# Ten Strassen pairs in place of seven, with the gates of four attention units among their blocks, and running states by scans

## The chip, the cores and the metric

The kernel runs on one core of a Trainium2 chip. The metric is the device time of one execution in microseconds. It was run three times: 1944.55, 1938.79 and 1942.80 us, median 1942.8. One further execution was profiled.

## The reference

One layer of a streaming encoder step is computed for a prompt of 1024 tokens and for 8 samples of 16 tokens, 1152 tokens in all (`NT`), with shared weights. The model width is 1024. Cut to what matters here:

```python
h = rms_norm(x, norm_g) * (1 + scale) + shift
proj = h @ w_in                       # one projection, 11296 columns
q, k, v, z_att, z_ssd, xbc, dt_raw, gates = split(proj)
q, k = rms_norm per head of 64
o_att = chunk-band attention (16 heads; own chunk of 64 + 8 chunks back; clipped relative bias)
att_branch = (o_att * silu(z_att)) @ w_att_proj
x, B, C = split(silu(causal_dwconv(xbc)))
for each chunk:                       # 32 heads of 64, 4 groups, state of 128
    y = (C B^T * decay) (x dt) + C h exp(a_cs)
    h = h * exp(a_cs_end) + B^T (x dt to_end)
ssd_branch = group_rms_norm((y + D x) * silu(z_ssd)) @ w_ssd_proj
merged = sigmoid(g_att) * att_branch + sigmoid(g_ssd) * ssd_branch
out = x + gate * (merged @ w_out)
```

The column ranges used below are `z_att` (1024 columns, 8 blocks of 128, one for each attention unit of two heads), `z_ssd` (2048 columns, 16 blocks, one for each pair of SSD heads) and `gates` (2048 columns, 16 blocks).

## The kernel before

All products are made in split single precision: an operand is a high part and a low part, and a product is three matmuls (high by high, high by low, low by high). A block of 128 columns of `w_in` for all tokens ("dense", the function `dense`) is 8 steps along the width x 3 groups of 384 tokens x 3 matmuls (L489, L490, L492) = 72 matmuls of 384 columns. The weights of a block arrive in one 512 KB load into one of two raw buffers (L350, issued by SyncE) and are split by ACT (high part, L374) and VectorE (low part, L375).

Two blocks can be made together by Strassen's scheme (`pairs`, with its weight forms in `w_form`): 7 products in place of 8 half-size ones, each with 24 matmuls of 288 columns (L880, L882, L883). `AHEAD_BLOCKS` lists the blocks that are made ahead of attention. The stages, in the order of time:

1. Start: normalisation, the conversion of the input into operands, the first block (`z_att` of unit 0) and four gate blocks dense (`NZ` = 5 blocks).
2. Seven pairs (`NPR`), the z blocks 0 to 13 of the SSD branch, then block 14 dense. Finished blocks go to HBM (`keep_block` into `z_d` or `gate_d`).
3. Eight attention units (`attention(u)`). A unit projects q, k and v token by token (`dense_tok`): 9 tiles of 128 tokens x 8 steps x 3 matmuls (L555 to L557), with 384 columns, in the last unit 416. The three weight pieces of a unit have one place: a piece's place comes free when the unit before has used it for the last time. Then comes one dense block, `z_att` of the next unit. The norms of q and k are made by POOL in three steps of 4, 4 and 1 token tiles (`prelude`: L1228, the Newton steps L328 to L334, and the product L1232), then the tiles are transposed on TensorE (L1252, L1268). Beside the projection of the next unit run the prompt rounds of this unit (scores L1390, transposes L1311, weighted sums L1334) and the sample's (L1443, L1446, L1470, L1480).
4. The SSD stage: four groups; in each a B and a C block with convolution, then four pairs of heads (`ssd(p)`). A pair has its x block (dense, convolution on VectorE, L1531), transposes L1754, eight chunk state products of 128x128 (L1799), the chain of running states, the in-chunk products (L1830) and those of the samples (L1837), the state output (L1855) and the sample's states (L1881). The chain of running states is fourteen operations of 64 columns on VectorE (L1808: state times decay plus the chunk's product; the first chunk is a copy on ACT, L1804), two for each chunk because a pair holds two heads. Seven further dense blocks are placed between pairs by the table `SLOTS` (z block 15 and gates 4 to 9).
5. The last six gate blocks, and the products with `w_att_proj`, `w_ssd_proj` and `w_out`.

What stands where is set in two steps. The program is written by generators: `run` lets the dense generators give a few matmuls at a time, counts the time that they are worth on a clock (`clock`, `credit`), and lets the other work in between, when its `pause` and `until` have passed. Then the Tile scheduler puts the instructions of each engine in an order by its own timeline. Instructions wrapped in `late` keep their program order. Each engine's queue is executed in order.

Of the kernel before, what the change touches and what calls it, by code (L numbers as in the profile page):

```python
# [12 lines left out]
P = 128  # L13
# [8 lines left out]
HD = 64  # L22
# [9 lines left out]
NEARLY = 15  # L32
SLOTS = (('p', 1), ('p', 3), ('p', 6), ('p', 9), ('p', 11), ('p', 13), ('p', 15))
BLOCKS = [("gate", i) for i in range(4)] + [("z", p) for p in range(NPAIR)] + [("gate", i) for i in range(4, 16)]
AHEAD_BLOCKS = BLOCKS[:4 + NEARLY]
FILL = dict(zip(SLOTS, BLOCKS[4 + NEARLY:]))
NGATE = 4 + NEARLY + len(SLOTS) - NPAIR
NZ = 5
NPR = 7
# [92 lines left out]
def trunk_kernel(ctx: ExitStack, tc: tile.TileContext, h):  # L132
# [118 lines left out]
    L_SSD = marena.set_layout(Z0, [("X", 1, XW), ("R", 2, 1184), ("t", 8, 36), ("pad", 1, 576), ("T", 9, NT), ("Y", 1, 1184), ("H", 1, 1024),  # L251
# [72 lines left out]
    z_d = drp.tile([1 + NPAIR, P, NT], F32, name="z_d")  # L324
# [17 lines left out]
    def job(*raw):  # L342
        jobs.append([len(parts) + i for i in range(len(raw))])
        parts.extend(raw)
# [119 lines left out]
    jobs_att = [len(jobs)]  # L464
    for u in range(NU - 1):
        job(*(h["wall"][nz + 4 * u + i] for i in range(3)))
        job(h["wall"][nz + 4 * u + 3])
    job(*(h["wlast"][i] for i in range(4)))
    jobs_att.append(len(jobs))
    for x in [h["wall"][i] for i in range(nz + 4 * NU - 4, 85)] + [h["watt"][i] for i in range(8)] + [h["wssd"][i] for i in range(16)] \  # L470
            + [h["wout"][i] for i in range(8)]:
        job(x)
# [538 lines left out]
    def keep_block(n, z):  # L1011
        what, i = AHEAD_BLOCKS[n - 1]
        dma(gate_d[i] if what == "gate" else z_d[1 + i], z.ap)
# [11 lines left out]
    def do(what, *x):  # L1025
        if what == "first":
            ev_z(z[0], late)(0, x[0], groups[x[0]], first[x[0]])
            if x[0] == 2:
                dma(z_d[0], z[0].ap)
                z[0].free()  # L1030
# [53 lines left out]
    def pause(t):  # L1084
        yield from until(clock[0] + t)
# [89 lines left out]
    def attention(u):  # L1175
# [4 lines left out]
        def dense_gen():  # L1180
            qk = yield from walloc(lay, "Q", 16 * P)
            if u == 0:
                turn = alloc(lay, "T", NT)
                z = zs[0] = alloc(lay, "T", NT)
                dma(z.ap, z_d[0])
                turn.free()
# [29 lines left out]
            yield from dense(hops, ev_z(z))  # L1216
# [329 lines left out]
    def dt_gen():  # L1546
# [36 lines left out]
        nc.scalar.activation(dec, pe[:, :256], AF.Exp)  # L1583
# [31 lines left out]
    ngate = [max(4, 4 + NEARLY - NPAIR)]  # L1615

    def fill_dense(*slot):
# [5 lines left out]
        def ev(o, g, tok, ps):  # L1623
# [3 lines left out]
            store(z_d[1 + i][:, tok], t.ap)  # L1627
# [57 lines left out]
    def ssd(p):  # L1685
# [7 lines left out]
        e4 = dec.rearrange("p (c e) -> p c e", e=32)  # L1693
# [43 lines left out]
        def main():  # L1737
# [54 lines left out]
            xm = [masked(0), masked(1)]  # L1792

            yield from pause(1500)
            for j in range(2):
                ps = pg()
                for s in range(4):
                    c = 4 * j + s
                    nc.tensor.matmul(ps[:, s * P:(s + 1) * P], tokb.ap[:, c * P:(c + 1) * P], xw.ap[:, c * P:(c + 1) * P],  # L1799
                                     start=True, stop=True)  # L1800
                for s in range(4):
                    c = 4 * j + s
                    if c == 0:
                        nc.scalar.activation(hst.ap[:, 0:P], ps[:, 0:P], AF.Copy)  # L1804
                        continue
                    for e in range(2):
                        o = c * P + e * HD
                        nc.vector.scalar_tensor_tensor(  # L1808
                            hst.ap[:, o:o + HD], hst.ap[:, o - P:o - P + HD], e4[:, c, 2 * p + e:2 * p + e + 1],
                            ps[:, s * P + e * HD:s * P + e * HD + HD], ALU.mult, ALU.add)  # L1810
                yield 4 * 213
                yield from pause(900)
            xw.free()
# [4 lines left out]
            yield from pause(1200)  # L1818
# [23 lines left out]
            dma(z.ap, z_d[1 + p])  # L1842
# [371 lines left out]
```

## Time and profile before

| | |
|---|---|
| runs | 1944.55, 1938.79, 1942.80 us; median 1942.8 |
| profiled execution | 1943.42 us, its span in the trace 1941.6 us |
| mean granted TensorE clock | 0.999 |
| HBM | 202.72 MB read, 53.68 MB written |

In the trace a start is counted from the start of the span. Busy time is the time in which an engine has at least one instruction in work. Matmuls are pipelined: the duration of one (some 340 ns with 384 columns) is longer than the step from one to the next, and it is the step that counts. A wait line reads: engine, tile and line that waited, the engine, tile and line waited for, the total in us, how many times, the longest. A group line reads: line, engine, operation, written tile, read tiles, shape, count, then busy time and mean ns of one, then idle time of the engine ahead of it and what ended it. A timeline line is start, duration, engine, line, operation. The window lines give length, then busy time and count for each engine asked for, granted clock, the DMA engines' busy share and GB/s. The trace counts a matmul of the language as one or two records (L1830 and L1334 two, the 384-column ones one).

### The profile page before, as it was taken

To read this page: it belongs to the slowest core of one execution; us is meant where nothing else is said; L and a number is where in the kernel's file an instruction comes from. 1 tells how busy PE (TensorE), PEld (TensorE's weight loads), DVE (VectorE), ACT (ScalarE), POOL (GpSimd) and SP (SyncE) were. 2 spreads that over 40 slices of the span, in tenths; PEclk is the share of its full clock that TensorE was granted. 3 is DMA by queue.
4 is the path that set the end of the run, shared out by engine and by line. 5 is a ranking of instruction groups with operands and counts; after the bars stand their busy time and mean duration, and the time that the engine had idled before them with its cause. 6 is when DMAs were issued, how large, how long until landed. Compare 5 with 4: busy or idle time off the path is not lost.

```text
span 1941.6 us, 35765 instructions
## 1 busy us (share of the span) xinstructions
PE 1922.7 (99%) x14259; PEld 1842.4 (95%) x14259; DVE 1251.5 (64%) x2577; ACT 798.3 (41%) x1639; POOL 339.7 (17%) x615
## 2 busy tenths in 40 slices
PE   7999999999999999999999999999999999999999
PEld 5999999999899998998999999999999999999999
DVE  6756634555556456558597988888885434777732
ACT  7533324444454444545655546465453311111200
POOL 0000003213123131221022343242241300000000
PEclk9999999999999999999999999999999999999999
DMA  8222342343333333423345354554558742331341
GB/s 316 92 81 95 109 173 69 96 129 116 97 117 101 122 116 94 130 82 115 119 132 181 132 162 152 168 173 140 160 192 289 292 144 93 105 105 56 89 143 52
DMA packets 85966, 258.73 MB, mean 133 GB/s; under 512 B 14732, under 2 KB 15768, under 8 KB 85800
## 3 DMA queue, kind: packets, MB, share of 16 engines
q1 hardware_dynamic: 77416, 229.57, 36.5%
q0 software_dynamic: 8384, 26.88, 3.6%
q8 instruction: 112, 1.84, 0.4%
q14 instruction: 54, 0.44, 0.1%
HBM read 202.72 MB, written 53.68 MB: 132 GB/s over the span
## 4 chain that ended last, share of the span: by engine, by line
PE 92%; DVE 3%; DMA 2%; ACT 1%; issue 1%; POOL 0%; SPq 0%; ACTq 0%; DVEq 0%; POOLq 0%
PE d L489 11%; PE d L492 11%; PE d L490 11%; PE d L557 5%; PE d L555 5%; PE d L556 5%; PE s L489 4%; PE s L490 4%; PE s L492 4%; PE g L1311 3%; PE g L1334 3%; PE s L1390 2%; PE g L880 2%; PE g L883 2%; PE g L882 2%; PE g L490 1%
## 5 line engine op out<-in xcount | busy, mean ns | idle before, releaser
L489 PE MATMUL d<-rarena 128*128 128x384 f32 x1288 | 437.7, 340 | 0.0
L492 PE MATMUL d<-rarena 128*128 128x384 f32 x1288 | 434.2, 337 | 0.0
L490 PE MATMUL d<-rarena 128*128 128x384 f32 x1288 | 433.3, 336 | 0.0
L489 PEld LDWEIGHTS d<-rarena 128*128 128x128 f32 x1288 | 242.0, 188 | 4.1 <-issue 2.7
L492 PEld LDWEIGHTS d<-rarena 128*128 128x128 f32 x1288 | 241.9, 188 | 2.2 <-issue 2.0
L490 PEld LDWEIGHTS d<-rarena 128*128 128x128 f32 x1288 | 242.1, 188 | 0.8 <-issue 0.4
L557 PE MATMUL d<-va_att,rarena 128*128 128x384 f32 (+1 forms) x567 | 197.6, 349 | 0.0
L555 PE MATMUL d<-va_att,rarena 128*128 128x384 f32 (+1 forms) x567 | 196.7, 347 | 0.0
L556 PE MATMUL d<-va_att,rarena 128*128 128x384 f32 (+1 forms) x567 | 193.7, 342 | 0.0
L374 ACT ACTIVATE rarena<-arena 128x1024 fp32r<-128x1024 f32 x76 | 80.5, 1059 | 262.9 <-PE s L490 173.9
L489 PE MATMUL s<-rarena 128*128 128x384 f32 x488 | 165.6, 339 | 0.0
L490 PE MATMUL s<-rarena 128*128 128x384 f32 x488 | 164.2, 336 | 0.0
L492 PE MATMUL s<-rarena 128*128 128x384 f32 x488 | 163.3, 335 | 0.0
L1299 ACT ACTIVATE ma_att<-ma_att 128x640 f32<-128x640 f32 (+2 forms) x144 | 101.5, 706 | 135.8 <-DVE ma_att L1408 99.7
L1228 POOL TENSOR_SCALAR ma_att<-ma_att 128x16 f32<-128x16 f32 (+1 forms) x24 | 5.2, 218 | 707.3 <-DVE ma_att L1205 417.2
L557 PEld LDWEIGHTS d<-va_att,rarena 128*128 128x128 f32 x567 | 107.0, 189 | 3.9 <-issue 2.7
L555 PEld LDWEIGHTS d<-va_att,rarena 128*128 128x128 f32 x567 | 106.8, 188 | 2.7 <-issue 1.2
L375 DVE TENSOR_TENSOR rarena<-arena,rarena 128x1024 fp32r<-128x1024 f32 x76 | 93.3, 1227 | 22.6 <-ACT rarena L374 22.6
L556 PEld LDWEIGHTS d<-va_att,rarena 128*128 128x128 f32 x567 | 106.8, 188 | 0.5
L1531 DVE SCALAR_TENSOR_TENSOR ma_att<-ma_att,arena 128x1176 f32<-128x1176 f32 x63 | 93.9, 1491 | 9.4 <-ACT ma_att L1528 8.1
L489 PEld LDWEIGHTS s<-rarena 128*128 128x128 f32 x488 | 91.7, 188 | 1.3 <-issue 1.2
L490 PEld LDWEIGHTS s<-rarena 128*128 128x128 f32 x488 | 91.7, 188 | 0.8 <-issue 0.8
(437 smaller groups left out, 4128.0 us busy)
## 6 DMA issues: line engine op xcount, KB each, us to landing
arena<-in_wall_dram SPq DMA_DIRECT2D x85, 512.0 KB, 3.6
ma_att<-in_kc_dram SPq DMA_DIRECT2D x64, 256.0 KB, 4.3
ma_att<-in_vc_dram SPq DMA_DIRECT2D x64, 256.0 KB, 3.5
ma_att<-acs_d SPq DMA_DIRECT2D x23, 576.0 KB, 6.8
ma_att<-y_d SPq DMA_DIRECT2D x15, 576.0 KB, 6.3
arena<-in_wssd_dram SPq DMA_DIRECT2D x16, 512.0 KB, 4.5
z_d<-va_start SPq DMA_DIRECT2D x13, 576.0 KB, 2.8
ma_att<-eacs_d SPq DMA_DIRECT2D x26, 288.0 KB, 3.9
```

What stands on the lines that cost most here:

```text
L374: keep(nc.scalar.activation(hi.r[:, c], b.ap, AF.Copy))
L375: keep(nc.vector.tensor_tensor(lo.r[:, c], b.ap, hi.ap[:, c], ALU.subtract))
L489: nc.tensor.matmul(ps, hi.r[:, wc], kh.r[:, tok], start=k == 0, stop=False)
L490: nc.tensor.matmul(ps, hi.r[:, wc], kl.r[:, tok], start=False, stop=False)
L492: nc.tensor.matmul(ps, lo.r[:, wc], kh.r[:, tok], start=False, stop=k == nk - 1)
L555: nc.tensor.matmul(ps, kh.r[:, tok], wh, start=j == 0, stop=False)
L556: nc.tensor.matmul(ps, kh.r[:, tok], wl, start=False, stop=False)
L557: nc.tensor.matmul(ps, kl.r[:, tok], wh, start=False, stop=j == KT - 1)
L1299: nc.scalar.activation(p, p, AF.Exp, bias=sm_[:, 4 + e:5 + e], scale=-1.0, accum_out=sm_[:, 6 + e:7 + e])
L1311: nc.tensor.transpose(ps[:, s * P:(s + 1) * P], p[:, (j + s) * P:(j + s + 1) * P], ident)
L1334: late(nc.tensor.matmul(po[e * HD:e * HD + HD, a * P:(a + 1) * P], v.ap[:, vc:vc + HD], x.ap[:, o + i * P:o + (i + 1) * P], start=i == 0, ...
L1531: nc.vector.scalar_tensor_tensor(yc, r.ap[:, j:j + n], w4[:, i, j:j + 1], yc, ALU.mult, ALU.add)
```

## The change

Blocks and order. The list of the blocks made ahead gets the `z_att` blocks of units 1, 3, 5 and 7 behind the four gates, and all sixteen z blocks follow. Ten pairs take the twenty blocks from index 5: the four unit gates and z blocks 0 to 15. One gate block (gate 4) is dense behind them. The unit gates are kept in `att_d`, the buffer of attention results, and the units 1, 3, 5 and 7 load theirs from there; the units before them (0, 2, 4 and 6) are then not followed by a dense block. Five slots in the SSD stage are left, for gates 5 to 9. The same six gates are left for the end. So there are six dense blocks fewer and three pairs more.

Running states. The decays are stored with the head outermost, and the decay of the first chunk is set to zero. All eight chunk products of a pair go to two PSUM banks. ACT copies them to SBUF with the chunk innermost (a write with a step of eight elements, two operations of 512 columns), makes for each head a tile of 512 decays by a broadcast, VectorE runs one `tensor_tensor_scan` of 512 for each head over state and chunk (the zero decay starts every row of eight anew), and ACT copies the result with a step of eight into the contiguous place `hst` from which the matmuls read it. The pauses are changed with it.

```diff
-NEARLY = 15
-SLOTS = (('p', 1), ('p', 3), ('p', 6), ('p', 9), ('p', 11), ('p', 13), ('p', 15))
-BLOCKS = [("gate", i) for i in range(4)] + [("z", p) for p in range(NPAIR)] + [("gate", i) for i in range(4, 16)]
+NPR = 10
+UNITS = (1, 3, 5, 7)
+SLOTS = (('p', 1), ('p', 3), ('p', 6), ('p', 10), ('p', 15))
+BLOCKS = [("gate", i) for i in range(4)] + [("unit", u) for u in UNITS] + [("z", p) for p in range(NPAIR)] + [("gate", i) for i in range(4, 16)]
+NAHEAD = 5 + 2 * NPR
...
-NPR = 7
...
-        dma(gate_d[i] if what == "gate" else z_d[1 + i], z.ap)
+        dma({"gate": gate_d, "z": z_d, "unit": att_d}[what][i], z.ap)
...
-            yield from dense(hops, ev_z(z))
+            if u + 1 in UNITS:
+                dma(z.ap, att_d[u + 1])
+            else:
+                yield from dense(hops, ev_z(z))
...
-        nc.scalar.activation(dec, pe[:, :256], AF.Exp)
+        d8 = dec.rearrange("p (e c) -> p e c", c=8)
+        nc.scalar.activation(d8, pe[:, :256].rearrange("p (c e) -> p e c", e=32), AF.Exp)
+        nc.vector.memset(d8[:, :, 0], 0.0)
...
+            dd = yield from walloc(lay, "D", 8 * HD)
+            def decays(e):
+                nc.scalar.activation(dd.ap[:, :8 * HD].rearrange("p (d c) -> p d c", c=8),
+                                     e4[:, 2 * p + e].unsqueeze(1).to_broadcast([P, HD, 8]), AF.Copy)
+            decays(0)
             yield from pause(1500)
+            ps2 = [pg(), pg()]
+            for c in range(8):
+                nc.tensor.matmul(ps2[c // 4][:, c % 4 * P:(c % 4 + 1) * P], tokb.ap[:, c * P:(c + 1) * P], xw.ap[:, c * P:(c + 1) * P],
+                                 start=True, stop=True)
+            xc = xw.ap[:, :NP].rearrange("p (n c) -> p n c", c=8)
             for j in range(2):
-                ps = pg()
-                for s in range(4):
-                    c = 4 * j + s
-                    nc.tensor.matmul(ps[:, s * P:(s + 1) * P], tokb.ap[:, c * P:(c + 1) * P], xw.ap[:, c * P:(c + 1) * P],
-                                     start=True, stop=True)
-                for s in range(4):
-                    c = 4 * j + s
-                    if c == 0:
-                        nc.scalar.activation(hst.ap[:, 0:P], ps[:, 0:P], AF.Copy)
-                        continue
-                    for e in range(2):
-                        o = c * P + e * HD
-                        nc.vector.scalar_tensor_tensor(
-                            hst.ap[:, o:o + HD], hst.ap[:, o - P:o - P + HD], e4[:, c, 2 * p + e:2 * p + e + 1],
-                            ps[:, s * P + e * HD:s * P + e * HD + HD], ALU.mult, ALU.add)
-                yield 4 * 213
+                nc.scalar.activation(xc[:, :, 4 * j:4 * j + 4], ps2[j].rearrange("p (c n) -> p n c", n=P), AF.Copy)
+            yield 8 * 213
+            yield from pause(1000)
+            hc = hst.ap[:, :NP].rearrange("p (c n) -> p n c", c=8)
+            for e in range(2):
+                hv = xw.ap[:, e * HD * 8:(e + 1) * HD * 8]
+                nc.vector.tensor_tensor_scan(hv, dd.ap[:, :8 * HD], hv, 0.0, ALU.mult, ALU.add)
+                if e == 0:
+                    decays(1)
+                nc.scalar.activation(hc[:, e * HD:(e + 1) * HD], xc[:, e * HD:(e + 1) * HD], AF.Copy)
                 yield from pause(900)
...
-            yield from pause(1200)
+            yield from pause(0)
```

Lines move: L374 and L375 become L376 and L377, L489 to L492 become L495 to L498, L555 to L557 become L561 to L563, L880 becomes L886, L1232 becomes L1241, L1252 and L1268 become L1261 and L1277, L1311 becomes L1320, L1334 becomes L1343, L1390 becomes L1399, L1470 and L1480 become L1479 and L1489, L1675 becomes L1686, L1830 and L1855 become L1848 and L1873, L1881 becomes L1899. New are L1807 (decays), L1815 (chunk products), L1819 (copies from PSUM), L1825 (scans) and L1828 (copies to `hst`).

Where it moves instructions. TensorE, at the end of unit 6's projection (`d_8043` its last token tile, `d_8088` the gate block of unit 7, the `g_` tiles transposes, weighted sums and sample sums of the unit before), before:

```order
L557 MATMUL d_8043<-va_att,rarena 128x384
L489 MATMUL d_8088<-rarena 128x384
L490 MATMUL d_8088<-rarena 128x384
L492 MATMUL d_8088<-rarena 128x384
L1311 MATMUL g_7895<-arena,ma_att 128x128
...
L1311 MATMUL g_7907<-arena,ma_att 128x128
L489 MATMUL d_8088<-rarena 128x384
L490 MATMUL d_8088<-rarena 128x384
L1334 MATMUL g_7916<-ma_att 64x128 x30
L1470 MATMUL g_7962<-ma_att 32x128 x20
```

The same place now (`d_8418` unit 6's last token tile, `d_8516` the first of unit 7, `s_8523` scores):

```order
L563 MATMUL d_8418<-va_att,rarena 128x384
L561 MATMUL d_8516<-va_att,rarena 128x416
L1320 MATMUL g_8270<-arena,ma_att 128x128
...
L1343 MATMUL g_8291<-ma_att 64x128 x30
L1479 MATMUL g_8337<-ma_att 32x128 x20
...
L1399 MATMUL s_8523<-rarena 128x128 x2
...
L1489 MATMUL g_8371<-arena,ma_att 128x128
L1261 MATMUL g_8461<-arena,ma_att 128x128 x4
L1261 MATMUL g_8468<-arena,ma_att 128x128 x4
L562 MATMUL d_8516<-va_att,rarena 128x416
L1277 MATMUL g_8489<-arena,ma_att 128x128 x2
```

Where the 72 matmuls of the gate block stood, the token matmuls of unit 7 stand, and the transposes of unit 6's last tokens (L1277) come after eleven of them.

TensorE, at the end of unit 0's projection, now (`d_3333` its last token tile, `d_3426` and `d_3508` the first two of unit 1):

```order
L563 MATMUL d_3333<-va_att,rarena 128x384
L561 MATMUL d_3426<-va_att,rarena 128x384
...
L1399 MATMUL s_3433<-rarena 128x128 x2
...
L563 MATMUL d_3426<-va_att,rarena 128x384
L561 MATMUL d_3508<-va_att,rarena 128x384
...
L563 MATMUL d_3508<-va_att,rarena 128x384
L561 MATMUL d_3426<-va_att,rarena 128x384
L561 MATMUL d_3508<-va_att,rarena 128x384
L562 MATMUL d_3426<-va_att,rarena 128x384
```

Before, the 72 matmuls of unit 1's gate stood behind the first of these rows. Now five of eight steps of the first tile stand there, then five of the second, and only then the steps that need the third weight piece.

VectorE, in pair 5 of the SSD stage (`g_11884` and `g_11903` its chunk products, L1848 the sum of x and the in-chunk output), before:

```order
L1808 SCALAR_TENSOR_TENSOR va_ssd<-va_ssd,ma_att,g_11884 128x64 x2
L1531 SCALAR_TENSOR_TENSOR ma_att<-ma_att,arena 128x1176
L1781 TENSOR_TENSOR rarena<-ma_att,rarena 64x128
L1808 SCALAR_TENSOR_TENSOR va_ssd<-va_ssd,ma_att,g_11884 128x64 x2
L1531 SCALAR_TENSOR_TENSOR ma_att<-ma_att,arena 128x1176
L1808 SCALAR_TENSOR_TENSOR va_ssd<-va_ssd,ma_att,g_11884 128x64 x2
L1848 SCALAR_TENSOR_TENSOR ma_att<-ma_att,arena,g_11936 128x512
L1531 SCALAR_TENSOR_TENSOR ma_att<-ma_att,arena 128x1176
L1808 SCALAR_TENSOR_TENSOR va_ssd<-va_ssd,ma_att,g_11903 128x64 x2
L1848 SCALAR_TENSOR_TENSOR ma_att<-ma_att,arena,g_11945 128x512
L1808 SCALAR_TENSOR_TENSOR va_ssd<-va_ssd,ma_att,g_11903 128x64 x6
L1848 SCALAR_TENSOR_TENSOR ma_att<-ma_att,arena,g_11954 128x128
```

And now (`g_12186` to `g_12204` the in-chunk products):

```order
L1792 TENSOR_TENSOR rarena<-ma_att,rarena 64x128
L1540 SCALAR_TENSOR_TENSOR ma_att<-ma_att,arena 128x1176
L1825 SCALAR_TENSOR_TENSOR va_ssd<-ma_att,va_ssd 128x512
L1540 SCALAR_TENSOR_TENSOR ma_att<-ma_att,arena 128x1176
L1866 SCALAR_TENSOR_TENSOR ma_att<-ma_att,arena,g_12186 128x512
L1825 SCALAR_TENSOR_TENSOR va_ssd<-ma_att,va_ssd 128x512
L1866 SCALAR_TENSOR_TENSOR ma_att<-ma_att,arena,g_12195 128x512
L1866 SCALAR_TENSOR_TENSOR ma_att<-ma_att,arena,g_12204 128x128
```

The fourteen operations, spread between the convolution's and the sums, have become two scans of 512.

39 lines of the change are left out of this document (23 added, 16 removed).

## The prediction

> **What bounds the kernel now.** I read the page's busy shares first, then its slices, then the shares of the chain that ended last, then TensorE's waits.
>
> ```profile
> PE 1922.7 (99%) x14259; PEld 1842.4 (95%) x14259; DVE 1251.5 (64%) x2577; ACT 798.3 (41%) x1639; POOL 339.7 (17%) x615
> PE   7999999999999999999999999999999999999999
> DVE  6756634555556456558597988888885434777732
> PE 92%; DVE 3%; DMA 2%; ACT 1%; issue 1%; POOL 0%; SPq 0%; ACTq 0%; DVEq 0%; POOLq 0%
> ```
>
> TensorE is busy for 1922.7 of 1941.6 us, and only the first slice is under 9. VectorE is near its limit only in the SSD stage, slices 21 to 31 or so. So an edit counts by the TensorE work that it adds or removes and by the waits that it leaves there. The waits of TensorE, by line waiting and line waited for:
>
> ```profile
> PE g L634 <- DMA m<-in_xT_dram: 8.5, 2, 8.3
> PE g L1881 <- POOL rarena L1788: 2.1, 2, 1.2
> PE g L1675 <- DVE ma_att L1537: 1.4, 1, 1.4
> PE g L1830 <- DVE ma_att L1808: 0.7, 1, 0.7
> PE g L1855 <- DVE ma_att L1848: 0.2, 1, 0.2
> ```
>
> 8.5 us of them is the start, which the change leaves alone. The last four rows, 2.1 + 1.4 + 0.7 + 0.2 = 4.4 us, lie in the SSD stage. Pairs and attention have none. The clock is full in every window below, so matmul counts can be turned into time.
>
> **Part 1: three more Strassen pairs.** Windows of TensorE alone inside dense blocks and inside pairs (length, busy time, count of matmuls, clock, DMA share, GB/s):
>
> ```profile
> 60.00:92.00 32.00, 32.00 (x186) 1.00 0.33 114
> 160.00:240.00 80.00, 80.00 (x603) 1.00 0.26 91
> ```
>
> An edge cuts about two matmuls of each count. 32.00 / 184 is 0.174 us for a matmul of 384 columns; 80.00 / 601 is 0.133 for one of 288. A pair of two blocks is 7 x 24 = 168 of the short ones, 22.4 us; two dense blocks are 2 x 72 = 144 long ones, 24.9 to 25.0. By the finer step that the starts of consecutive dense matmuls give (0.1733), six dense blocks fewer are 6 x 72 x 0.1733 = 74.9 us, and three pairs more 3 x 168 x 0.1332 = 67.2 us. That is **-7.7 us**. All other matmuls are the same in number. The 80 us window is full, so ten pairs in a row should run as seven do: their operand sums lie on the other engines, beside TensorE. The number of weight blocks is the same; four blocks of attention gate more go to HBM and come back, and at a DMA share of 0.26 to 0.33 I cost that at nothing. If it were not hidden, a late block would show as a wait of an attention unit's output product on the load of its gate, a whole unit after the load was issued; so I take it as hidden.
>
> **Part 2: four attention units follow each other with no dense block between.** In the order, the block between units 0 and 1, 2 and 3, 4 and 5, 6 and 7 is gone (12.5 us of cover each). Three things lay under it: the third weight piece of the next unit, the norms of the last tokens on POOL with the transposes behind them, and the refill of buffers. Units 0 to 1, by the timeline:
>
> ```profile
> 309.59 0.34 PE L557 MATMUL d<-va_att,rarena 128*128 128x384 f32 x1
> 309.76 0.34 PE L489 MATMUL d<-rarena 128*128 128x384 f32 x1
> 309.71 1.89 SPq L350 DMA_DIRECT2D arena<-in_wall_dram  x2
> 313.37 1.06 ACT L374 ACTIVATE va_att<-arena 128x1024 fp32r<-128x1024 f32 x1 [2.68 <-DMA arena<-in_wall_dram]
> 314.46 2.30 DVE L375 TENSOR_TENSOR va_att<-arena,va_att 128x1024 fp32r<-128x1024 f32 x1 [2.69 <-ACT va_att L374]
> 313.77 1.91 POOL L1232 TENSOR_TENSOR ma_att<-ma_att 128x1024 f32<-128x1024 f32 x1
> 319.98 0.61 POOL L1232 TENSOR_TENSOR ma_att<-ma_att 128x256 f32<-128x256 f32 x1
> 318.12 1.04 PE L1252 MATMUL g<-arena,ma_att 128*128 128x128 f32 x8
> ```
>
> The third piece is loaded at 309.71, when unit 0's last matmul starts, is split by ACT from 313.37, and its low half is done by VectorE at 314.46 + 2.30 = 316.76. Before, dense matmuls ran from 309.76 meanwhile. Now the next unit's matmuls start there. The scheduler has moved the blocks that need piece 3 back: ahead of the first one that needs its low half stand, in the changed order, 32 token matmuls and 12 score matmuls (rows with the prices of the latter, and of others that stand between units):
>
> ```profile
> 324.59 1.06 PE s L1390 x12
> 389.04 3.43 PE g L1334 x60
> 392.47 1.23 PE g L1470 x40
> ```
>
> 32 x 0.173 + 1.06 = 6.6 us, so 316.4 against 316.8: **a wait of 0.4**. The last transposes stand 10.4 to 10.8 us in, and the norm that they read ends at 319.98 + 0.61 = 320.59, 10.8 us in: 0 to 0.4. Between 2 and 3 and between 4 and 5 the same count leaves about 2 us to spare: nothing. Between 6 and 7:
>
> ```profile
> 786.66 0.34 PE L557 MATMUL d<-va_att,rarena 128*128 128x384 f32 x1
> 796.37 0.61 POOL L1232 TENSOR_TENSOR ma_att<-ma_att 128x256 f32<-128x256 f32 x1
> ```
>
> The norm ends at 796.98, 10.15 us after the last token matmul hands over (786.66 + 0.17). Ahead of the transposes stand now 11 token matmuls of 416 columns (0.188 each, scaled from 0.1733), 15 other transposes (eight take 1.04 by L1252's row, less where they follow each other; 0.12 each, 1.8), the weigh products of 3.43 and 1.23 and 12 scores (1.06): 9.6 us. **A wait of 0.5.** With up to 0.3 for a projection buffer whose eviction is late I take **+1.2 us** for the four places together; 0 from below, since no work is removed that TensorE had waited for, and 2 from above by the same counts. The wait holds up everything behind it on TensorE, whose queue is in order.
>
> The rest of the four units' work loses 12.5 us of cover too. A whole unit, by engine:
>
> ```profile
> 403.90:484.35 80.45, 80.45 (x690) 74.22 (x689) 45.81 (x143) 37.52 (x91) 18.85 (x37) 1.00 0.36 112
> ```
>
> (PE, weight loads, DVE, ACT, POOL.) VectorE's 45.8 us fit in 80.45 - 12.5 = 68 us with a third to spare, so I cost this at nothing.
>
> **Part 3: running states by scans.** What goes and the nearest rows for what comes (groups by shape: busy time and mean ns):
>
> ```profile
> L1808 DVE SCALAR_TENSOR_TENSOR ma_att<-ma_att,g 128x64 f32<-128x64 f32 x168 | 35.7, 273 | 4.8 <-ACT ma_att L1804 2.6 <-PE g L1799 2.0
> L1808 DVE SCALAR_TENSOR_TENSOR va_ssd<-va_ssd,ma_att,g 128x64 f32<-128x64 f32 x56 | 12.2, 274 | 0.9 <-PE g L1799 0.8
> L1848 DVE SCALAR_TENSOR_TENSOR ma_att<-ma_att,arena,g 128x512 f32<-128x512 f32 x26 | 19.1, 742 | 2.9 <-PE g L1830 2.8
> L1531 DVE SCALAR_TENSOR_TENSOR ma_att<-ma_att,arena 128x1176 f32<-128x1176 f32 x63 | 93.9, 1491 | 9.4 <-ACT ma_att L1528 8.1 <-DMA ma_att<-in_h_dram 0.7
> L1804 ACT ACTIVATE ma_att<-g 128x128 f32<-128x128 f32 x12 | 3.3, 274 | 15.9 <-PE g L1799 10.8 <-DMA out_hs_dram<-ma_att 5.1
> L1313 ACT ACTIVATE ma_att<-g 128x512 f32<-128x512 f32 x96 | 54.8, 591 | 13.7 <-PE g L1311 13.1
> 1040.00:1480.00 440.00, 435.53 (x3379) 425.96 (x3378) 378.84 (x627) 233.26 (x489) 140.66 (x230) 1.00 0.52 167
> 1190.87 2.12 PE g L1830 x36
> 1192.99 0.89 PE g L1837 x32
> ```
>
> VectorE loses (35.7 + 12.2) / 16 = 3.0 us per pair of heads. It gains two scans of 512. No row shows a scan, in which each element needs the one before it; the bounds are 0.74 (512 elements, L1848) and 1.49 (L1531, 2.3 times the elements). I take 1.1, halfway, since nothing tells which row is nearer: 2.2 per pair, 0.8 less than before. ACT gets two evictions, two decay broadcasts and two copies of 512 at 0.59 and loses one 0.27 piece: 3.3 us per pair, 52 in all, beside 233.26 busy of 440. None of this is TensorE's. It matters by the chain from the last state matmul (L1815) to the first state output (L1873): eviction 0.59, scan 1.1, decays for the second head 0.59 once the first scan has freed their buffer, scan 1.1, copy 0.59 are 4.0 us; with hand-overs and the work that stands between on both engines I count 4.7 to 6.7. On TensorE the changed order leaves more than that: for pair 5, 32 dense matmuls (5.5 us), the 36 in-chunk ones (2.12) and the sample ones (0.89) make 8.6; over the 16 pairs it is 5.7 to 10.2, mean 8.4. So no wait from it. The 0.7 us that L1830 waited for VectorE's old chain goes: **-0.7 us**. The two dense blocks that leave the SSD stage (five in place of seven) are in part 1; without their 25 us VectorE has 378.8 - 11 us of work in 415, 89% where it was 86%.
>
> ACT writes and reads the states with a step of eight elements. The row of 591 ns is contiguous in SBUF, and with eviction and copy at twice that row the chain is 5.9 to 7.9 us, still under 8.4. The Trainium skill ("SBUF — State Buffer", Specifications (TRN2)) says that SBUF wants at least two hits on a 16-byte line for full bandwidth and that each crossing to a new line costs; here every element would lie in a line of its own. It gives no figure; no run here shows such an access yet, so its sum is the same or, where the price is high, that of rival C.
>
> **Sum.** 1943.4 - 7.7 + 1.2 - 0.7 = 1936.2 on the profiled execution, which took 1943.42 us (span 1941.6), 0.6 above the median of the runs. Against the median: **1935.6 us**.
>
> **Rivals.** *A, the SSD waits go too.* The pauses and the mix of work at L1881 and L1675 change, and VectorE has less per pair. If the other 3.7 us of waits there vanish: 1935.6 - 3.7 = 1931.9. Against it: the order has the same distance between the group's c block and L1675 as before, and 89% of VectorE is tighter.
>
> *B, the joints between units cost more.* VectorE's split of piece 3 took 2.30 us at the first joint and can take 2.90:
>
> ```profile
> 468.10 2.90 DVE L375 TENSOR_TENSOR va_att<-arena,va_att 128x1024 fp32r<-128x1024 f32 x1 [1.24 <-ACT va_att L374]
> ```
>
> If it also queues behind one softmax operation, or if the norms on POOL (a chain of some 10 us from the last token matmul at both joints counted) start a microsecond later, each joint waits 1.2 to 2 us more: 5 to 8 in all, 1940.6 to 1943.6, say 1942, and the gain is spent. For it: the margins at two joints are already below zero.
>
> *C, slower: the running states come late.* Place: L1873 behind L1815 in each of 16 pairs. It decides from a chain of 8.4 us on; below 5.7 no pair waits. If the scans and the two strided operations of the chain cost three times their rows (0.74 and 0.59), the sequence above is 2 x 1.77 + 0.59 + 2 x 2.22 = 8.6 us, and with the same 0.7 to 2.7 for hand-overs 9.3 to 11.3, 10.3 in the middle: 1.9 x 16 = 30, so 1966. At 2.2 times it is about 8 us; then only the short spacings wait, some 8 us in all, 1943. Against it: the margin of 2 us at the prices taken.
>
> **How the numbers follow.** 0.3% of the median, which is about what a measurement of this kernel can tell from no change, is 5.8 us: faster is below 1937.0, slower above 1948.6. The forecast case has 0.50, its own range is 1933 to 1939 (joints at 0 or 4, SSD waits partly gone), so 0.32 of it is faster and 0.18 the same. A has 0.20, all faster. B has 0.18, all the same. C has 0.12, of which 0.10 is slower and 0.02 the same. Together 0.52, 0.38, 0.10. The range leaves out the slow part of C and a little at A's end, where A and joints without waits would give 1930.7: 1930 to 1946.
>
> **What would show it.** Right: a pairs stretch with no TensorE wait at 0.133 us per matmul; waits of at most 1 us at the joints of units 0-1 and 6-7, on POOL's L1241 or VectorE's L377; no wait of L1873 on the copies at L1828; the waits on POOL's L1799 and VectorE's L1546, the new numbers of L1788 and L1537, as before. Wrong: a scan above 1.5 us or a copy above 1.2, with L1873 waiting in most pairs (C); four waits of over 1 us at the joints (B); DMA as what ends a wait at the attention units' gates or in the pairs, which I have costed at nothing.

## The result and the profile after

The changed kernel took 1973.61 us (median of 4 runs, 1973.22 to 1975.83) against 1942.38 before: a ratio of 1.0158, 95% interval 1.0145 to 1.0172. It is 31 us slower, outside the range of the prediction. The profiled execution has a span of 1974.1 us, 32.5 more than before.

Where the time went is read by stage first. Windows of TensorE from the first matmul of the pairs to the first of attention, to the first of the SSD stage's groups (L1669, now L1680), to the end (length, busy time, count, clock, DMA share, GB/s), before:

```profile
102.30:271.40 169.10, 169.10 (x1250) 1.00 0.33 114
271.40:962.40 691.00, 691.00 (x5759) 1.00 0.34 107
962.40:1941.60 979.20, 971.14 (x6684) 1.00 0.45 149
```

After:

```profile
101.00:337.20 236.20, 236.20 (x1754) 1.00 0.33 111
337.20:990.60 653.40, 651.72 (x5473) 1.00 0.35 113
990.60:1974.10 983.50, 956.70 (x6539) 0.99 0.44 146
```

The pairs took 67.1 us more, as three pairs should (67.2), with no wait. Attention lost four dense blocks, 49.9 us of work, and became only 37.6 shorter: 12.3 us are missing there. The SSD stage and the end lost two dense blocks, 24.95 us, and became 4.3 us longer: 29.3 us are missing there. With the 1.3 us that the start happened to be shorter, 67.1 - 37.6 + 4.3 - 1.3 is the 32.5.

TensorE's busy time of the whole page rose, though it has 7.7 us less work:

```profile
PE 1934.5 (98%) x14331; PEld 1842.2 (93%) x14331; DVE 1255.8 (64%) x2434; ACT 867.1 (44%) x1737; POOL 333.1 (17%) x609
```

The waits of TensorE now (the line that waited, the line waited for, total, times, longest):

```profile
PE g L1899 <- POOL rarena L1799: 11.5, 11, 2.1
PE g L640 <- DMA m<-in_xT_dram: 8.8, 2, 8.5
PE g L1873 <- ACT ma_att L1828: 4.6, 3, 2.7
PE g L1873 <- ACT va_ssd L1828: 3.4, 3, 1.4
PE g L1765 <- DVE ma_att L1546: 1.4, 1, 1.4
```

The state output L1873 waits for the copies six times, 8.0 us in all, at the one place that the prediction had looked at. The larger wait, 11.5 us, is at the sample's states L1899, for POOL's masked products, which wait in turn for VectorE's L1792 and for the matmuls. Idle time in the SSD stage and the end together rose from 979.20 - 971.14 = 8.1 to 983.50 - 956.70 = 26.8 us. And the clock there is 0.99. At one of the waits, us by us:

```profile
1061.00:1062.00 1.00, 1.00 (x9) 1.00 0.00 0
...
1067.00:1068.00 1.00, 0.11 (x1) 1.00 0.13 12
1068.00:1069.00 1.00, 0.50 (x2) 1.00 0.00 0
1069.00:1070.00 1.00, 0.25 (x2) 1.00 0.48 197
1070.00:1071.00 1.00, 1.00 (x7) 0.79 0.26 106
1071.00:1072.00 1.00, 1.00 (x5) 0.50 1.06 406
1072.00:1073.00 1.00, 1.00 (x5) 0.50 0.90 230
1073.00:1074.00 1.00, 1.00 (x5) 0.51 0.93 373
1074.00:1075.00 1.00, 1.00 (x8) 1.00 0.01 0
```

TensorE waited twice, 2.1 us in all, and then ran for some 3.4 us at half the clock: the losses of the four rows below 1.00 are 0.21 + 0.50 + 0.50 + 0.49 = 1.7 us. There are five such stretches in the SSD stage now, 8.5 us, and none before. They count as busy time, which is why the busy share hides them.

Beside this stands a wait of VectorE, on the load of the chunk decays (`eacs_d`, into the buffer `eb`). Before:

```profile
DVE va_ssd L1861 <- DMA va_ssd<-eacs_d: 2.9, 1, 2.9
DVE ma_att L1861 <- DMA ma_att<-eacs_d: 1.6, 2, 1.2
```

After:

```profile
DVE ma_att L1879 <- DMA ma_att<-eacs_d: 36.6, 10, 7.8
DVE va_ssd L1879 <- DMA va_ssd<-eacs_d: 18.0, 4, 7.1
```

4.5 us became 54.6. How much of the loss this makes is for the experiments; one pair in the timeline shows how it comes about (pairs are counted from 0). Before, pair 6 (state products on TensorE, the load issued by SyncE, the product that needs it on VectorE):

```profile
1187.20 1.05 PE L1799 MATMUL g<-ma_att 128*128 128x128 f32 x8
1188.29 1.09 SPq L1816 DMA_DIRECT2D ma_att<-eacs_d  x2
1197.64 0.28 DVE L1861 TENSOR_TENSOR ma_att<-ma_att,g 128x128 f32<-128x128 f32 x1
```

After, pair 5 (chunk products, copies from PSUM, scan, copy to `hst`, scan, copy, load, product):

```profile
1193.79 0.94 PE L1815 MATMUL g<-va_ssd,ma_att 128*128 128x128 f32 x7
1194.77 1.09 ACT L1819 ACTIVATE va_ssd<-g 128x512 f32<-128x512 f32 x2 [1.32 <-PE g L1815]
1196.52 1.22 DVE L1825 TENSOR_TENSOR_SCAN va_ssd<-ma_att,va_ssd 128x512 f32<-128x512 f32 x1
1198.30 1.11 ACT L1828 ACTIVATE va_ssd<-va_ssd 128x512 f32<-128x512 f32 x1
1199.64 1.21 DVE L1825 TENSOR_TENSOR_SCAN va_ssd<-ma_att,va_ssd 128x512 f32<-128x512 f32 x1
1200.89 1.15 ACT L1828 ACTIVATE va_ssd<-va_ssd 128x512 f32<-128x512 f32 x1 [0.50 <-DVE va_ssd L1825]
1202.07 1.09 SPq L1834 DMA_DIRECT2D va_ssd<-eacs_d  x2
1210.00 1.35 DVE L1879 TENSOR_TENSOR va_ssd<-va_ssd,g 128x384 f32<-128x384 f32 x3 [7.11 <-DMA va_ssd<-eacs_d]
```

`eb` takes the place of the weighted x, `xw`. Before, `xw` was read last by the state products: the load was issued right behind them, 0.3 us after the last one starts in most pairs. Now the copies from PSUM are written into `xw`, the scans work in it, and the last copy to `hst` reads it. The load waits for that: it is issued 8.0 us after the last state product, mean of the 16 pairs (5.8 to 12.6), and VectorE stands at L1879: in the 7.1 us ahead of it in this pair it starts nothing else, and the next pair's convolution, masks and sums come behind it.

### The profile page after: what moved, and what is told of

Same layout as the page of the kernel before. It is cut to its first block, busy times and chain, and to the rows that moved or that the text cites. A ratio compares the mean times of both kernels' runs of the same rounds, so it can differ in the third digit from the quotient of the medians.

```text
span 1974.1 us, 35921 instructions
## 1 busy us (share of the span) xinstructions
PE 1934.5 (98%) x14331; PEld 1842.2 (93%) x14331; DVE 1255.8 (64%) x2434; ACT 867.1 (44%) x1737; POOL 333.1 (17%) x609
## 5 line engine op out<-in xcount | busy, mean ns | idle before, releaser
L495 PE MATMUL d<-rarena 128*128 128x384 f32 x1160 | 394.6, 340 | 0.0
L498 PE MATMUL d<-rarena 128*128 128x384 f32 x1160 | 392.6, 338 | 0.0
L496 PE MATMUL d<-rarena 128*128 128x384 f32 x1160 | 392.0, 338 | 0.0
L495 PEld LDWEIGHTS d<-rarena 128*128 128x128 f32 x1160 | 219.0, 189 | 1.9 <-issue 1.5
L498 PEld LDWEIGHTS d<-rarena 128*128 128x128 f32 x1160 | 219.1, 189 | 1.5 <-issue 0.9
L496 PEld LDWEIGHTS d<-rarena 128*128 128x128 f32 x1160 | 219.2, 189 | 0.6 <-issue 0.2
L561 PE MATMUL d<-va_att,rarena 128*128 128x384 f32 (+1 forms) x567 | 197.1, 348 | 0.0
L563 PE MATMUL d<-va_att,rarena 128*128 128x384 f32 (+1 forms) x567 | 196.9, 347 | 0.0
L376 ACT ACTIVATE rarena<-arena 128x1024 fp32r<-128x1024 f32 x70 | 74.0, 1058 | 241.0 <-PE s L496 157.2
L495 PE MATMUL s<-rarena 128*128 128x384 f32 x472 | 161.3, 342 | 0.0
L496 PE MATMUL s<-rarena 128*128 128x384 f32 x472 | 159.8, 339 | 0.0
L498 PE MATMUL s<-rarena 128*128 128x384 f32 x472 | 159.4, 338 | 0.0
L561 PEld LDWEIGHTS d<-va_att,rarena 128*128 128x128 f32 x567 | 106.9, 189 | 4.7 <-issue 3.7
L563 PEld LDWEIGHTS d<-va_att,rarena 128*128 128x128 f32 x567 | 106.9, 189 | 3.3 <-issue 1.4
L377 DVE TENSOR_TENSOR rarena<-arena,rarena 128x1024 fp32r<-128x1024 f32 x70 | 86.6, 1237 | 20.4 <-ACT rarena L376 20.2
L495 PEld LDWEIGHTS s<-rarena 128*128 128x128 f32 x472 | 89.6, 190 | 0.9 <-issue 0.8
L496 PEld LDWEIGHTS s<-rarena 128*128 128x128 f32 x472 | 89.7, 190 | 0.4 <-issue 0.4
```

What stands on the lines that cost most here:

```text
L376: keep(nc.scalar.activation(hi.r[:, c], b.ap, AF.Copy))
L377: keep(nc.vector.tensor_tensor(lo.r[:, c], b.ap, hi.ap[:, c], ALU.subtract))
L495: nc.tensor.matmul(ps, hi.r[:, wc], kh.r[:, tok], start=k == 0, stop=False)
L496: nc.tensor.matmul(ps, hi.r[:, wc], kl.r[:, tok], start=False, stop=False)
L498: nc.tensor.matmul(ps, lo.r[:, wc], kh.r[:, tok], start=False, stop=k == nk - 1)
L561: nc.tensor.matmul(ps, kh.r[:, tok], wh, start=j == 0, stop=False)
```

## The experiments

Theory **L**: the load that comes late is the main loss. Rival **C**: the longer chain itself (scans, strided copies) decides, as in the prediction. For attention, theory **J**: the missing dense blocks at the four joints cost it. Ratios are against the kernel before on the same chip.

**e1_pairs: the blocks alone.** The changed kernel with the hunks of the running states (L1590 to L1594, L1704, L1804 to L1836) put back as before.

> Only the blocks are changed (ten pairs, unit gates, five slots); the running states go by the fourteen old operations. Theory L (late load: the scans hold the place of the weighted x until the last copy, so the load of the chunk decays that takes its place comes late, VectorE stands at it for 55 us in all and TensorE behind VectorE): VectorE's waits on eacs_d fall under 10 us, the SSD waits of TensorE fall from 24 to under 8 us, the half-clock stretches go; 1973.6 - 20 - 8.5 = 1945. Theory S (the two slots that left the SSD stage are what makes it tight, whatever the running states are): waits of over 15 us stay, 1960 or more. On the joints between attention units both leave the 12 to 13 us that attention lost in the changed kernel.

1949.89 us, 1.0036 (1.0022 to 1.0050): 5 over the 1945 of theory L, 10 under theory S. The block part alone is 7 us slower, not 7.7 faster. Its attention and what follows:

```profile
338.00:990.40 652.40, 651.14 (x5471) 1.00 0.35 113
990.40:1948.20 957.80, 947.06 (x6539) 1.00 0.46 150
```

957.8 against the 983.5 with the scans: 25.7 us are the scans' in these two profiled executions, 23.7 by the medians (1973.61 - 1949.89). Against 979.2 - 24.95 = 954.25 only 3.6 are missing, with one wait of 4.7 us for POOL and a spell at half clock behind it, so the two slots that left cost little here. Attention is as short of its mark as with the scans. VectorE waits 10.4 us for `eacs_d`, where theory L had under 10.

**e2_scans: the scans alone**, in the kernel before.

> Only the running states are changed; seven pairs, unit blocks and seven slots as before. Theory L: the load of the chunk decays is issued some 8 us after the last state product in place of 0.3, VectorE waits for it 35 to 55 us in all; TensorE loses 15 to 29 us with its slow clock stretches: 1957 to 1971. Theory S: with the seven slots the same chain is covered, 1943 to 1948. Attention takes 691 us as before.

1955.23 us, 1.0070 (1.0055 to 1.0085); SSD stage and end 996.2 us, 17.0 more than before. VectorE waits 38.3 us for the load. Slightly under the range of theory L: the scans cost less here (12.7 us by the medians, 23.7 beside the ten pairs). That the two slots more cover the difference fits, but no run separates it.

**e3_eb_in_mask: the load into another place.**

```diff
-            xw.free()
-            eb = alloc(lay, "T", NT)
-            for e in range(2):
-                dma(eb.ap[e * HD:(e + 1) * HD], eacs_d[...])
...
             for t in me + [xd]:
                 t.free()
+            eb = alloc(lay, "T", NT)
+            for e in range(2):
+                dma(eb.ap[e * HD:(e + 1) * HD], eacs_d[...])
             z = alloc(lay, "T", NT)
+            xw.free()
```

> The changed kernel, but the load of the chunk decays (eacs_d) takes the place of the first mask, which comes free after the in-chunk products, not that of the weighted x, which the last copy frees. Theory L: the load is issued 3 to 4 us sooner, VectorE's wait on it falls from 55 to 10 to 30 us and the time falls by 5 to 18: 1956 to 1968. Theory C (rival C alone: the state output waits for the strided copies): the waits of L1873 on the copies stay at 8 us and those of the sample's states too; 1970 to 1976.

1960.17 us, 1.0091 (1.0077 to 1.0105): 13.4 us less than the changed kernel. VectorE's wait fell to 35.4 us:

```profile
DVE va_ssd L1879 <- DMA va_ssd<-eacs_d: 33.0, 9, 7.2
DVE ma_att L1879 <- DMA ma_att<-eacs_d: 2.4, 2, 1.6
```

Both are short of what was expected. The issue moved forward by only 1.2 us in the mean (3 to 4 were expected): by 2.3 to 7.5 us in seven pairs, and it came later in six; L1879 starts 14.1 us after the last state product in place of 14.6. So this run does not tell what an early load is worth. No half-clock stretch is left in the SSD stage, and L1873 waits for the copies 4.9 us in place of 8.0. In the profiled executions these stretches are 8.5 of the 17.6 us between the changed kernel and this one. SSD stage and end took 965.9 us, and all that it has over e1 is idle time:

```profile
990.60:1956.50 965.90, 946.93 (x6539) 1.00 0.45 149
```

965.90 - 946.93 = 19.0 against 957.80 - 947.06 = 10.7 in e1.

**e4_before_late: the load made late.** In the kernel before, one small copy on ACT that reads the last running state and writes `xw`, ahead of the point where `xw` is given up:

```diff
+            nc.scalar.activation(xw.ap[:, NP:NP + 64], hst.ap[:, 7 * P + HD:], AF.Copy)
             xw.free()
             eb = alloc(lay, "T", NT)
```

> The kernel before, with one thing added: ahead of the point where the weighted x is given up, a copy of 64 columns on ACT reads the last running state, so that the load of the chunk decays is issued some 6 us after the last state product in place of 0.3. The running states themselves are as before. Theory L: VectorE waits for the load 20 to 45 us in all, TensorE's waits in the SSD stage rise from 4 to over 12 us, 1949 to 1962. Theory C: the load does not matter, 1941 to 1945.

1956.34 us, 1.0077 (1.0062 to 1.0093). VectorE's waits, with the fourteen old operations untouched:

```profile
DVE ma_att L1862 <- DMA ma_att<-eacs_d: 37.7, 12, 5.2
DVE va_ssd L1862 <- DMA va_ssd<-eacs_d: 14.7, 3, 6.4
```

52.4 us of wait and 14 us of time, without a half-clock stretch, with the load issued 8.3 us after the last state product in the mean of pairs 0 to 14 (3.4 to 13.8; the last pair's load is early, as it was before). This one edit costs as much as the scans do in the same kernel (e2, 12.7 us). A late load is thus enough for a loss of that size. One thing comes with it: the added copy waits for the last running state too, and ACT stands at it for 20.9 us in all. Of TensorE's waits in the SSD stage only one, of 1.3 us, names ACT, so this is likely a small part, but no run takes it away.

**e5_early and e7_scans_early: the load before the state products.** In 12 of 16 pairs (0 to 8 and 10 to 12 in e5, 0 to 7 and 10 to 13 in e7) `eb` takes the fill blocks' staging place, which is free there, and is loaded ahead of L1815; `xw` is kept as long as `eb`, so nothing else gets more room. e5 does it in the changed kernel, e7 in e2.

> The changed kernel, but in 12 of the 16 pairs (1 to 12) the load of the chunk decays is issued ahead of the state products, into a place of its own that the fill blocks' staging leaves free; the weighted x is kept as long as the loaded decays, so that nothing else gets more room. Theory L: VectorE's wait on eacs_d falls from 55 to under 15 us, TensorE's waits on the sample's states from 11.5 to under 5, the slow clock stretches go; what the longer chain costs by itself (8 us at the state output) may stay: 1950 to 1958. Theory C (the chain itself decides): 1962 to 1974.

> As e2 (seven pairs, the scans), with the early load of e5. Theory L: the 13 us that the scans cost go for the most part: 1942 to 1948, VectorE's wait on eacs_d under 10 us, no half-clock stretch. Theory C: 1951 to 1957 as e2.

e5: 1960.86 us, 1.0091 (1.0075 to 1.0108). e7: 1952.63 us, 1.0052 (1.0038 to 1.0065). VectorE's waits for the load are down to 9.7 and 11.2 us. In e5:

```profile
DVE va_ssd L1889 <- DMA va_ssd<-eacs_d: 5.3, 1, 5.3
DVE ma_att L1889 <- DMA ma_att<-eacs_d: 4.4, 2, 3.1
```

e5 is 12.7 us faster than the changed kernel but over its range, with two spells at half clock left, 1297 to 1308 and 1444 to 1452; e7 gains only 2.6 on e2 where 7 to 13 were expected, with intervals that overlap. So beside ten pairs about half of the scans' 23.7 us goes with the late load, and beside seven pairs most of their cost stays when VectorE's wait for the load is gone. The costs do not add: e4 has such a wait and loses 14 us by it, e7 has the scans without it and is still 9 us over the kernel before. With the load early, L1879 (L1889 here) still starts 11.2 us (e5) after the last state product, against 8.6 in e1; that the state output behind the copies is later would explain it, which no run shows by itself.

**e9_contig: copies without a step,** on top of e3. `nc.scalar.activation(hst.ap[:, e * HD * 8:(e + 1) * HD * 8], hv, AF.Copy)` in place of the copy with a step. The state then lies chunk innermost, so the outputs that use it are not the layer's.

> As e3, but ACT's two copies per pair read with no step (the state then lies in the wrong order, chunk innermost, and the outputs that use it are not the reference's); the first chunks then depend on the first copy alone. Theory C (what is left of the scans' cost is the price of the strided copies): a copy falls from 1.12 to about 0.6 us, the 4.9 us that the state output waits for copies fall under 2.5, 1952 to 1957. Theory R (the rest is the work and the order behind it, not the copies): 1957 to 1962.

1957.93 us, 1.0076 (1.0061 to 1.0091), 2.2 less than e3; its own four runs spread over 7.5 us, so this is not clear of noise. In e3 and in e9 the copies took:

```profile
L1828 ACT ACTIVATE ma_att<-ma_att 128x512 f32<-128x512 f32 x16 | 17.9, 1122 | 4.0 <-DVE ma_att L1825 4.0
```

```profile
L1828 ACT ACTIVATE ma_att<-ma_att 128x512 f32<-128x512 f32 x16 | 10.0, 624 | 7.2 <-DVE ma_att L1825 7.2
```

The wait of L1873 for copies fell from 4.9 to 1.0 us; two spells at half clock, some 4.5 us, came back behind other waits and hide a part of what it gains. The price of the step is real, half a microsecond for each copy, and it is not what most of the rest consists of.

**e10_hp_act, e13_mask_hp, e14_early_hp: POOL's stand at a store.** POOL issues the store of the last state (L1835) and waits there for the last copy, 89 us in all, with the masked products behind it. In e10 ACT issues that store (`nc.scalar.dma_start`), e13 and e14 add it to e3 and e5.

> The changed kernel, but the store of the last state is issued by ACT, which makes the copies, not by POOL. Theory P (POOL stands at that store until the last copy, 89 us in all, with the masked products behind it): the 11.5 us that TensorE waits for the masked products fall under 4, 1962 to 1968. Theory L (they are late because VectorE is): the waits stay over 8 us, 1970 to 1976.

> e3 and e10 together: the load of the chunk decays in the first mask's place and the store of the last state issued by ACT. If the load and POOL's stand at the store are two separate costs, the 4.6 us of e10 come off the 1960.2 of e3: 1953 to 1958, 4 to 8 us over e1. If POOL's stand matters only because VectorE is late too: 1958 to 1963.

> e5 and e10 together: the early load in 12 of 16 pairs and the store of the last state issued by ACT. Separate costs: 1954 to 1958. Otherwise 1959 to 1964.

e10: 1969.01 us, 1.0128 (1.0115 to 1.0142); the waits for the masked products fell from 11.5 to 6.6, between the two theories. e13: 1962.50, e14: 1960.02 us: with the load's place changed, taking POOL's stand away brings nothing that can be seen. No second cost of its own shows.

**e6_gates and e8_early_gates: gates 4 to 7 in the pairs, not unit gates** (`UNITS = ()`), with the old running states (e6) and with e5 (e8). All units keep their dense block; two gates in place of six are left at the end.

> As e1 (old running states, ten pairs, five slots), but the four extra blocks of the pairs are gates 4 to 7, not the gates of attention units; every attention unit is followed by its dense block as before, and two gates in place of six are left at the end. Theory J (the 11 us that attention lost come from the missing dense blocks at four joints): attention takes 691 us again, e1 less 11: 1936 to 1940. Rival (the dense blocks at the end are cover too: with two gates the loads and splits of the attention results come late): waits of over 8 us behind the SSD stage, 1944 to 1952.

> e5 and e6 together: ten pairs with gates 4 to 7, scans, early load. If both theories hold and the parts add: 1973.6 - 20 - 11 = 1938 to 1946. If the end of the SSD stage lacks cover: 1948 to 1956.

e6: 1977.14 us, 1.0168 (1.0149 to 1.0187); e8: 1990.29 us, 1.0242 (1.0224 to 1.0261). Both are over both of their ranges. Attention in e6:

```profile
337.70:1028.70 691.00, 691.00 (x5759) 1.00 0.33 106
```

691.0 again, to a tenth: theory J is shown. But the end has lost cover, and by more than the rival had allowed for. The first product with the attention results (L495) waits for ACT's split of them (L1936):

```profile
PE g L495 <- ACT rarena L1936: 18.5, 3, 14.2
```

and between 1518 and 1553 the clock is at half for most of the time.

**e11_nine, e12_eight, e15_eight_six: fewer pairs, no unit gates,** old running states. e11: nine pairs, five slots, four gates at the end. e12: eight pairs (z blocks only), five slots, six gates. e15: eight pairs, six slots, five gates.

> Old running states, nine pairs (z blocks 0 to 15, gates 4 and 5), gate 6 dense, the unit blocks dense as before, five slots, four gates left at the end. Theory J and the cover at the end: two pairs more are worth 2 x 2.56 = 5.1 us, attention takes 691 us, and four gates cover the loads and splits that two did not (14 us of wait in e6 against 25 us more cover): 1936 to 1941. Rival: the end still lacks cover: 1943 to 1955.

> As e11 with eight pairs (z blocks only), gate 4 dense, gates 5 to 9 in the five slots, six gates left at the end as before. One pair more is worth 2.6 us; the SSD stage with five slots costs up to 3.6: 1939 to 1944 if the end needs no more cover than six gates, and 2 to 3 us more than e11 if four gates are enough.

> As e12 (eight pairs of z blocks, old running states, unit blocks dense), with six slots in the SSD stage (p = 1, 3, 6, 9, 11, 15) and five gates left at the end. If the 4 us that the SSD stage of e12 has over its work come from the missing slots: 1939 to 1942. If five gates are too few at the end: 1945 to 1952.

e11: 1958.11 us, 1.0073 (1.0061 to 1.0085), over its rival's range too: 7.3 us of wait for ACT's split, and the clock at half at 1527 to 1534 and from 1557 on, near the end of the SSD stage. e12: 1944.16 us, 1.0005 (0.9997 to 1.0014), no difference. e15: 1945.66 us, 1.0018 (1.0007 to 1.0029). So two and four gates at the end are too few. For five it is open: e15 has no wait for ACT's split (L1936), and its interval overlaps that of e12. Six slots are no better than five. No version beat the kernel before.

## Why the prediction was wrong, point by point

**Pairs: right.** -74.9 + 67.2 us of work; the stage took 67.1 us more, full.

**The step that failed is the one that priced part 3**: "None of this is TensorE's. It matters by the chain from the last state matmul (L1815) to the first state output (L1873)." The chain was followed to its consumer on TensorE only. It has a second end: the place that it works in. `xw` was held 8 us longer, the load into it came 8 us later, VectorE stood for 55 us, and the sample's states, the next pair's work and the state output came late with it. By the medians, some 7.3 of the 31 us are the blocks' (e1) and 23.7 the scans' beside them. Of these 23.7 us, an early load takes away 12.7 (e5), and a late load added to the kernel before costs 14 (e4). e3 won 13.4 us, but it hardly moved the load, and about half of what it won in the profiled executions (8.5 of 17.6 us) are the half-clock stretches that are gone, so it is no second measure of the same thing. In the kernel with seven pairs the early load took away only 2.6 of 12.7 us (e7); why so little, no run shows. What is left beside ten pairs, some 11 us, is for the most part idle time at several lines (8.3 us more than e1 in e3), none of which accounts for it alone; the step of the copies (e9) and POOL's stand at the store (e13, e14) were tried, and neither is most of it. It stays open how it divides.

None of the signs that the prediction had named for being wrong came: scan and copy stayed under 1.5 and 1.2 us, L1873 waited six times and not in most pairs, no wait in attention was over 1 us, and none there or in the pairs ended with a DMA. Those that spoke of the scans looked at the chain and its consumer on TensorE alone.

**Prices of part 3.** In the changed kernel:

```profile
L1825 DVE TENSOR_TENSOR_SCAN ma_att<-ma_att 128x512 f32<-128x512 f32 x22 | 26.8, 1220 | 8.3 <-ACT ma_att L1819 5.8 <-ACT ma_att L1807 2.4
L1819 ACT ACTIVATE ma_att<-g 128x512 f32<-128x512 f32 x22 | 11.9, 592 | 9.6 <-PE g L1815 9.6
L1828 ACT ACTIVATE ma_att<-ma_att 128x512 f32<-128x512 f32 x18 | 20.2, 1124 | 3.8 <-DVE ma_att L1825 3.8
```

Scan 1.22 us where 1.1 was taken; copies from PSUM 0.59, as taken; copies to `hst` 1.12 where 0.59 was taken; decays 0.63. The step is not where the prediction and the account of the change put it. Both views of a copy run with the chunk innermost, and the trace's operands have the copy to `hst` read its 512 elements in one run and write them as 64 times 8, each of the eight into another chunk, 128 elements on. The copy from PSUM reads with that step of 128 and writes runs of four elements. So neither reads SBUF with a step of eight, and it is the write of single elements far apart that is dear. The chain came to 8.0 us in the mean where 4.7 to 6.7 was counted, 5.9 to 7.9 with strided prices on both. That the state output waits at L1873 at all comes from this.

**Part 2 was mis-sized.** +1.2 us was taken; e6 against e1 gives 11.3 (691.0 - 49.9 = 641.1 against 652.4). The visible waits were as priced: the span of attention in e1 has 652.40 - 651.14 = 1.3 us of idle time. The rest has no wait row. Two units in the middle, from the first token matmul of unit 2 to that of unit 4, before and in e1:

```profile
403.68:564.57 160.89, 160.89 (x1378) 1.00 0.36 111
```

```profile
460.77:611.45 150.68, 150.68 (x1306) 1.00 0.37 118
```

72 matmuls fewer should be 12.48 us and are 10.21, with TensorE busy all through in both: 2.3 us are in longer steps. At the first joint it is 3.0, at the last one, with what follows it, 3.8. The score matmuls grew most: their busy time in all of attention, with 624 of them in each, before and in e1:

```profile
271.40:962.40 691.00, 57.90 (x624) 1.00 0.34 107
```

```profile
338.00:990.40 652.40, 65.06 (x624) 1.00 0.35 113
```

In the two units they stand in 16 pieces between other matmuls where they stood in 10, and the step out of a piece takes some 0.25 us where one inside takes 0.08. Busy time counts the tail of each piece too; from start to start, the score matmuls take 6.0 us more in all of attention (61.0 against 55.0), in 63 pieces where they stood in 41, the transposes L1320 3.4 and the token matmuls 2.5. So the added pieces of the scores, 22 x 0.17 = 3.7 us, are a third of the 11.3, and the rest is spread. That the cuts into more pieces are the cause is argued from the steps, not shown by a run. Rival B had the place right and put 5 to 8 us where 11.3 were lost, by the wrong means: it spoke of late weight pieces and norms.

**Rival C** had the sign, and by luck nearly the total (1966), since its place was wrong: 8.0 us at L1873 where it put 30. Its chance of 0.12 was too low, since the margin of 2 us that spoke against it was that of one consumer.

**The clock was not in the sum at all.** 8.5 us of the 31 are half-clock stretches behind waits: a wait of 1.35 us at 1410 cost 3.1 with the 1.7 behind it.

**Small terms.** The wait on L1808 went (-0.7) and does not matter beside the rest. That the attention gates can be loaded at no cost held: no wait of TensorE names those loads.

## What to carry to other kernels

When an operation is moved into a buffer that used to be free early, follow the buffer, not only the data: look up what is allocated in its place next, when that load can now be issued, and what stands behind the instruction that needs it. A dense block that looks like plain work is also cover, at the joints between units and at the end; take blocks out where the stage behind does not need their time, and count what is left (six gates at the end were enough here, four and two were not). When the time grows and the waits do not explain it, compare stage lengths, then the granted clock, then the step of one kind of matmul.

## What the runs showed of the hardware

Half-clock stretches came after short waits. In the changed kernel a single wait of 1.51 us at 1266 and two of 1.09 and 1.05 us at 1067 to 1070 were each followed by some 3.4 us at half the clock, at a cost of 1.7 us; waits of 2.13 us at 1182 and 2.69 us at 1376 were not. The Trainium skill ("TensorE: Matmul & The Clock Gate", Part 1: The HAM clock gate) has the clock halve after an idle window of about 3.4 us and come back after a busy one of that length, and has the window run free of the kernel. The length of the stretches agrees with it; that so short a wait brings one does not, and the measurement decides. Why a longer wait can pass without one, no run here shows.

ACT copied 512 fp32 elements from SBUF to SBUF in 1.12 us when each write went 128 elements on from the last, against 0.62 with reads and writes in one run (e9). Reading PSUM with that step and writing SBUF in runs of four took 0.59, as long as the copies of 512 without a step in the kernel before (L1313). A scan of 512 took 1.22 us where a product and sum of the same size took 0.74.
